# Attention's first gate projection ahead of the convolution's pointwise product, with TensorE's order planned from other durations

## The chip, the cores and the metric

The kernel runs on one core of one Trainium2 chip. The metric is the device time of one execution in microseconds, as the median of several runs; smaller is better.

## What is computed

A decoder trunk of two layers, on 256 positions of width 2048, all in float32. Each layer normalises its input, multiplies it by one combined projection matrix, and sends the columns of the result to three branches: a convolution module of 512 channels, a gated DeltaNet of 6 heads and a dilated windowed attention of 12 heads. Every branch has a gate of its own. The gated outputs together go through one output projection, which is added to the input.

```python
for l in range(DEPTH):
    h = rms_norm(x, norm_w[l])
    u = h @ w_in[l].astype(h.dtype)
    (c_in, c_gate, g_q, g_k, g_v, g_z, g_b, g_a,
     a_q, a_k, a_v, a_gate) = jnp.split(u, cuts, axis=-1)
    y_conv = conformer_conv(c_in, ..., conf_pw_w[l]) * jax.nn.silu(c_gate)
    y_gdn = gated_deltanet(g_q, g_k, g_v, g_z, g_b, g_a, ...)
    y_att = dilated_attention(a_q, a_k, a_v, cos, sin) * jax.nn.silu(a_gate)
    y = jnp.concatenate([y_conv, y_gdn, y_att], axis=-1)
    x = x + y @ w_out[l].astype(y.dtype)
return rms_norm(x, final_norm_w)

def conformer_conv(u, dw_w, dw_b, ln_w, ln_b, pw_w):
    a, b = jnp.split(u, 2, axis=-1)
    h = a * jax.nn.sigmoid(b)
    h = causal_dwconv(h, dw_w) + dw_b.astype(h.dtype)   # 31 taps
    h = layer_norm(h, ln_w, ln_b)
    h = jax.nn.silu(h)
    return h @ pw_w.astype(h.dtype)
```

The last line of `conformer_conv` is the pointwise product: 512 channels by 512. The DeltaNet's chunked rule solves a triangular system for each chunk of 64 positions (the kernel builds that inverse step by step, in the tile `inv`) and carries a state from chunk to chunk.

## The kernel before

**Projections.** Nearly all of TensorE's work is projection matmuls. Every float32 operand is split into a high and a low part, and a product is made of three matmuls (high by high, low by high, high by low). The normalised input lies in `HT` (high in HT0, low in HT1), 16 blocks of 128 channels; the input of the output projection and of the pointwise product lies in `YT` in the same way. Weights come by DMA on SyncE's queue into `raw` (4 buffers). ScalarE makes their high part `whi`, VectorE the low part `wlo` = raw - whi; each of these has 3 buffers. `unit` emits the matmuls of one block of 128 channels, 6 of them, or three for each 128 output columns in the channel-wise jobs ("chan"), in which the weights are the moving operand's partner and a matmul has 256 columns.

**Jobs.** `project` is one task that walks a list of jobs in a fixed order, the same in both layers: first the DeltaNet's and the convolution's input columns, then attention's q, k and v (AQ0 to AV1, of 384 columns each), the convolution's gate CG (512 columns), and at the layer's end the pointwise product and attention's two gate projections AG0 and AG1 (384 columns each, 144 matmuls); then the pieces of the output projection. A job accumulates in a pair of PSUM banks `acc`, of which there are two pairs, and when it is done a task is started that takes the result further (`conv_gate`, `conv_out`, `att_gate`).

**The convolution's chain.** Its taps run on VectorE as `scalar_tensor_tensor` instructions, one per tap and 128 channels (line 196 of the helper that records them). Then TensorE transposes the result, ScalarE and VectorE make mean and variance over channels (`lnst`), VectorE normalises, TensorE transposes back (tiles `b512_0` and `b512_1`), and ScalarE and VectorE apply scale, shift and swish and write the split result to the first four blocks of YT, in two halves of two blocks. Only then is the event `conf["pw"]` set, for which the pointwise product waits. The transposes are recorded at line 239 (`trs`), the other small matmuls of the chains at line 232 (`mms`).

**What sets the order.** All of it is written by generators ("tasks") that yield operations with an estimated duration: `("pe", cost, emit)` and so on. `Plan.run` is a list scheduler: it keeps a clock per engine, and of all the tasks' next operations it emits the one that can start first by the estimates, then by priority. The chip executes each engine's instructions in exactly this order; semaphores do the waiting. So the estimates decide where between the projection's matmuls the chains' small matmuls stand, and where between the weight splits VectorE's other instructions stand. The estimate's core is

```python
start = max(self.clock[o[0]], t.ready(o[0]))
key = (start, t.prio)
if best is None or key < best[0]:
    best = (key, t, o)
```

## Time and profile before

| what | value |
|---|---|
| median of 3 runs | 982.55 us (981.98 to 984.06) |
| the profiled execution's own time | 983.13 us |
| its span, first to last instruction | 981.4 us |
| mean granted TensorE clock | 0.991 |
| TensorE busy, matmuls | 959.3 us, 98% |
| VectorE busy | 758.6 us, 77% |
| ScalarE busy | 544.7 us, 56% |
| GpSimd busy | 57.4 us, 6% |

The span is that of one profiled execution; some 1.7 us of its time lie around it. The share of an engine is an average over the whole span: an engine at 77% can be full for a hundred microseconds and half empty elsewhere. A matmul's duration in the trace includes its way through the array, so that consecutive ones overlap; the pace is read from their starts. The granted clock is a share of 2.4 GHz, at its two levels 1.00 and 0.50 (1.2 GHz).

### The profile page before, as it was taken

The numbers are of one execution on the slowest core, as the hardware profiler recorded it, in microseconds if no ns is written. First come the engines' busy times: TensorE is split into PE (matmuls) and PEld (weight loads), VectorE is DVE, ScalarE is ACT, GpSimd is POOL, SyncE is SP. The second block draws the span as 40 slices with busy tenths as digits, with TensorE's granted clock in tenths as the row PEclk, the third lists the DMA queues.
The fourth block names the chain that finished last, engine by engine and source line by source line (L and its number), as shares of the span: only waits on it lengthen the run. The fifth ranks groups of instructions, "written<-read, shape, count | busy, mean of one in ns | idle before, by whom it ended". The sixth has DMA issues, their size and how long they took to land.

```text
span 981.4 us, 19748 instructions
## 1 busy us (share of the span) xinstructions
PE 959.3 (98%) x7595; PEld 937.9 (96%) x7595; DVE 758.6 (77%) x1473; ACT 544.7 (56%) x1061; POOL 57.4 (6%) x79
## 2 busy tenths in 40 slices
PE   8999999999999989999999999999999999899996
PEld 8999999999999979999899999999999999799996
DVE  7686799997999856655558768999989996666672
ACT  8764356445675665454456633564456656645551
POOL 1002000200110000000000020002001200100000
PEclk9999999999999979999999999999999999999998
DMA  9765555644445525777666555656344564467772
GB/s 335 255 215 155 184 192 181 187 145 148 150 141 186 186 65 181 223 241 222 215 200 198 197 163 172 192 179 199 124 142 152 163 201 148 131 194 222 228 251 86
DMA packets 67502, 180.31 MB, mean 184 GB/s; under 512 B 8016, under 2 KB 12240, under 8 KB 67408
## 3 DMA queue, kind: packets, MB, share of 16 engines
q1 hardware_dynamic: 64752, 174.08, 55.1%
q0 software_dynamic: 1712, 3.28, 1.3%
q10 hardware_dynamic: 944, 1.70, 0.5%
q8 instruction: 59, 0.97, 0.4%
q14 instruction: 35, 0.29, 0.1%
HBM read 173.26 MB, written 4.98 MB: 182 GB/s over the span
## 4 chain that ended last, share of the span: by engine, by line
PE 60%; DVE 1%; ACT 1%; issue 1%; ACTq 0%; POOLq 0%; POOL 0%; DVEq 0%
PE acc L454 54%; PE mix L232 3%; PE mix L239 2%; PE acc L463 1%; ACT b L191 0%; DVE b L196 0%; DVE wlo L199 0%; ACT JUNK L191 0%; ACT whi L191 0%; ACT YT L191 0%; DVE YT L199 0%; PE mix L753 0%; DVE inv L212 0%; DVE b L199 0%; ACTq L1064 0%
## 5 line engine op out<-in xcount | busy, mean ns | idle before, releaser
L454 PE MATMUL acc<-HT,whi 128*128 128x256 f32 x3072 | 541.7, 280 | 0.0
L191 ACT ACTIVATE whi<-raw 128x768 fp32r<-128x768 f32 (+4 forms) x389 | 340.1, 875 | 361.7 <-PE acc L454 311.2
L199 DVE TENSOR_TENSOR wlo<-raw,whi 128x768 fp32r<-128x768 f32 (+4 forms) x389 | 384.6, 989 | 167.1 <-ACT whi L191 163.6
L454 PEld LDWEIGHTS acc<-HT,whi 128*128 128x128 f32 x3072 | 466.4, 188 | 2.3 <-issue 1.8
L454 PE MATMUL acc<-HT,wlo 128*128 128x256 f32 x1536 | 426.7, 278 | 0.0
L454 PEld LDWEIGHTS acc<-HT,wlo 128*128 128x128 f32 x1536 | 288.6, 188 | 0.0
L454 PE MATMUL acc<-whi,YT 128*128 128x384 f32 (+2 forms) x640 | 161.8, 336 | 0.0
L196 DVE SCALAR_TENSOR_TENSOR b<-b,par,b 128x255 f32<-128x255 f32 (+20 forms) x348 | 151.9, 463 | 0.3
L454 PE MATMUL acc<-whi,HT 128*128 128x384 f32 (+1 forms) x512 | 134.6, 344 | 0.6 <-ACT whi L191 0.6
L454 PEld LDWEIGHTS acc<-whi,YT 128*128 128x128 f32 x640 | 114.0, 188 | 2.4
L454 PE MATMUL acc<-wlo,YT 128*128 128x384 f32 (+2 forms) x320 | 107.5, 336 | 0.0
L454 PEld LDWEIGHTS acc<-whi,HT 128*128 128x128 f32 x512 | 91.8, 190 | 1.3 <-ACT whi L191 1.2
L454 PE MATMUL acc<-wlo,HT 128*128 128x384 f32 (+1 forms) x256 | 87.2, 341 | 0.4 <-DVE wlo L199 0.4
L454 PEld LDWEIGHTS acc<-wlo,YT 128*128 128x128 f32 x320 | 60.1, 188 | 1.4
L454 PEld LDWEIGHTS acc<-wlo,HT 128*128 128x128 f32 x256 | 48.3, 189 | 1.1 <-DVE wlo L199 0.9
L232 PE MATMUL mix<-b,b 128*128 128x128 f32 (+5 forms) x456 | 47.3, 291 | 1.4 <-ACT b L191 1.4
L239 PE MATMUL mix<-ident,b 128*128 128x128 f32 x232 | 39.4, 290 | 7.2 <-DVE b L208 3.6
L232 PEld LDWEIGHTS mix<-b,b 128*128 128x128 f32 (+3 forms) x456 | 36.5, 163 | 8.6 <-ACT b L191 2.9
L239 PEld LDWEIGHTS mix<-ident,b 128*128 128x128 f32 x232 | 28.3, 147 | 11.2 <-DVE b L208 4.0
L191 ACT ACTIVATE b<-mix 128x384 f32<-128x384 f32 (+3 forms) x70 | 29.4, 436 | 16.9 <-PE mix L232 9.0
L196 DVE SCALAR_TENSOR_TENSOR b<-b,b 128x256 f32<-128x256 f32 (+3 forms) x62 | 31.5, 510 | 5.5 <-ACT b L191 5.4
L191 ACT ACTIVATE JUNK<-b 128x128 bf16<-128x128 f32 (+3 forms) x62 | 25.0, 403 | 16.2 <-DVE b L199 11.0
(148 smaller groups left out, 642.1 us busy)
## 6 DMA issues: line engine op xcount, KB each, us to landing
raw<-in_w_in SPq DMA_DIRECT2D x240, 384.0 KB
raw<-in_w_in SPq DMA_DIRECT2D x48, 512.0 KB
raw<-in_w_out SPq DMA_DIRECT2D x64, 384.0 KB
raw<-in_w_out SPq DMA_DIRECT2D x12, 512.0 KB
raw<-in_w_in SPq DMA_DIRECT2D x15, 396.0 KB
b<-in_x SPq DMA_DIRECT2D x10, 256.0 KB
raw<-in_conf_pw_w SPq DMA_DIRECT2D x4, 512.0 KB
raw<-in_w_out SPq DMA_DIRECT2D x8, 256.0 KB
```

The source lines that it names most:

```text
L191: lambda: nc.scalar.activation(out_, in_, func, bias=bias, scale=scale, **kw))
L196: lambda: nc.vector.scalar_tensor_tensor(out_, a, s, b, op0=op0, op1=op1))
L199: return ("dve", 70 + _free(out_) / 0.96, lambda: nc.vector.tensor_tensor(out_, a, b, op=op))
L232: nc.tensor.matmul(o, a, b, start=f[0], stop=f[1])
L239: nc.tensor.transpose(o, a, ident)
L454: nc.tensor.matmul(o, w, m, start=first and i == 0 and not (chan and t % 2), stop=last and i == 2, skip_group_check=chan)
L463: nc.tensor.matmul(acc[t][:, :n], YT[w][:, k, s], HT[m][:, k, :n], start=k == 0 and i == 0, stop=k == KB - 1 and i == 2)
```

## The change

Two things are changed. In the job list, attention's gate projection AG0 moves ahead of the pointwise product, so that a layer ends with CG, AG0, pointwise product, AG1, where it had CG, pointwise product, AG0, AG1. And the estimated durations of TensorE's operations are other ones: a projection unit of 384 columns counts 1035 or 1038 ns where it counted 975, a transpose costs 109 ns and 100 for the group where it cost 107, and a group of small matmuls is estimated by its columns and partitions. Nothing of what is computed changes, nor the number of instructions.

```diff
--- before.py
+++ after.py
@@ -230,14 +230,18 @@
             for o, a, b, *f in jobs:
                 f = f or (True, True)
                 nc.tensor.matmul(o, a, b, start=f[0], stop=f[1])
-        cost = sum(max(53.0, 4 * max(_free(j[1]), _free(j[2])) / 2.4) for j in jobs)
-        return ("pe", cost, emit)
+        def one(a, b):
+            n = max(_free(a), _free(b))
+            if n <= 64:
+                return 30.0 if n <= 32 else 58.0
+            return 2 * n / 2.4 * (0.5 if min(a.shape[0], _free(a)) <= 64 else 1.0) + 4.0
+        return ("pe", 100.0 + sum(one(j[1], j[2]) for j in jobs), emit)
 
     def trs(*jobs):
         def emit():
             for o, a in jobs:
                 nc.tensor.transpose(o, a, ident)
-        return ("pe", 107.0 * len(jobs), emit)
+        return ("pe", 100.0 + 109.0 * len(jobs), emit)
 
     def summax(out_, a, b, mx):
 
@@ -453,7 +457,7 @@
                 for i, (w, m) in enumerate(terms):
                     nc.tensor.matmul(o, w, m, start=first and i == 0 and not (chan and t % 2), stop=last and i == 2,
                                      skip_group_check=chan)
-        return ("pe", 6 * (n / 2.4 + 2.5), emit)
+        return ("pe", n // 128 * 3 * 115.0 if chan else 6 * (n / 2.4 + 13.0), emit)
 
     def last_unit(acc, t, k, n):
 
@@ -462,7 +466,7 @@
             for i, (w, m) in enumerate(((0, 0), (1, 0), (0, 1))):
                 nc.tensor.matmul(acc[t][:, :n], YT[w][:, k, s], HT[m][:, k, :n], start=k == 0 and i == 0,
                                  stop=k == KB - 1 and i == 2)
-        return ("pe", 3 * (n / 2.4 + 2.5), emit)
+        return ("pe", 3 * (n / 2.4 + 13.0), emit)
 
     def project(jobs):
 
@@ -1264,9 +1268,9 @@
             inp(AV + 384 * i, 384, heads_in(i), 7)
         inp(CG, 512, conv_gate, 6, True)
         cs_ready = [conf["pw"]] * KB
+        inp(AG, 384, att_gate(0), 6, True)
         jobs.append((YT, cs_ready, wpw, 0, 512, full[:2], conv_out, 6, None, True))
-        for i in range(2):
-            inp(AG + 384 * i, 384, att_gate(i), 6, True)
+        inp(AG + 384, 384, att_gate(1), 6, True)
         for j, (c0, n) in enumerate(pieces):
             mode = "last" if last and j == len(pieces) - 1 else False
             jobs.append((YT, y_ready, wout, c0, n, [(4 * i, 4) for i in range(4)] if mode else full, (last_residual if last else residual)(j),
```

Since the estimates set the order, the change moves instructions on all engines. Three places are shown.

TensorE, end of layer 0, before: the group of transposes of `b512_0` and `b512_1` (the normalised convolution output) that stands last ahead of the pointwise product, whose matmuls read YT0 and YT1. Ahead of these rows stand the transposes of the first half, and ahead of them CG's last matmul.

```order
L232 MATMUL mix3_126<-b384_2_111,b768_1_91 64x256
L232 MATMUL mix3_126<-b384_3_112,b768_1_91 64x256
L232 MATMUL mix3_126<-b384_2_111,b768_1_91 64x128
L232 MATMUL mix3_126<-b384_3_112,b768_1_91 64x128
L239 MATMUL mix2_125<-ident_139,b512_0_107 128x128
L239 MATMUL mix2_125<-ident_139,b512_1_108 128x128
L239 MATMUL mix2_125<-ident_139,b512_0_107 128x128
L239 MATMUL mix2_125<-ident_139,b512_1_108 128x128
L454 MATMUL acc10_129<-YT0_76,whi2_85 128x256
L454 MATMUL acc10_129<-YT1_77,whi2_85 128x256
L454 MATMUL acc10_129<-YT0_76,wlo2_88 128x256
```

After the change, the transposes stand inside AG0 (matmuls that read HT), the first group 63 of its 144 matmuls in, the second group 117 in:

```order
L458 MATMUL acc11_130<-HT1_75,whi2_85 128x256
L458 MATMUL acc11_130<-HT0_74,wlo2_88 128x256
L243 MATMUL mix2_125<-ident_139,b512_0_107 128x128
L243 MATMUL mix2_125<-ident_139,b512_1_108 128x128
L243 MATMUL mix2_125<-ident_139,b512_0_107 128x128
L243 MATMUL mix2_125<-ident_139,b512_1_108 128x128
L458 MATMUL acc10_129<-HT0_74,whi2_85 128x256
L458 MATMUL acc10_129<-HT1_75,whi2_85 128x256
```

```order
L458 MATMUL acc11_130<-HT1_75,whi2_85 128x256
L458 MATMUL acc11_130<-HT0_74,wlo2_88 128x256
L243 MATMUL mix1_124<-ident_139,b512_0_107 128x128
L243 MATMUL mix1_124<-ident_139,b512_1_108 128x128
L243 MATMUL mix1_124<-ident_139,b512_0_107 128x128
L243 MATMUL mix1_124<-ident_139,b512_1_108 128x128
L458 MATMUL acc10_129<-HT0_74,whi2_85 128x256
```

and the pointwise product begins right behind AG0's last matmul:

```order
L458 MATMUL acc11_130<-HT0_74,whi0_83 128x256
L458 MATMUL acc11_130<-HT1_75,whi0_83 128x256
L458 MATMUL acc11_130<-HT0_74,wlo0_86 128x256
L458 MATMUL acc00_127<-YT0_76,whi1_84 128x256
L458 MATMUL acc00_127<-YT1_77,whi1_84 128x256
L458 MATMUL acc00_127<-YT0_76,wlo1_87 128x256
```

What moved: the pointwise product stands 144 matmuls further behind CG, and between the second group of transposes and its first matmul there are now 27 of AG0's matmuls where there was none.

VectorE, middle of layer 1, before: weight splits (`wlo`), steps of the DeltaNet's inverse (`inv` and the product `b_3` beside it, 48 partitions, at the steps of 16 to 14 rows) and taps of the short convolution (`b_5`, `par`):

```order
L199 TENSOR_TENSOR wlo_86<-raw_81,whi_83 128x768
L199 TENSOR_TENSOR b_3_118<-inv_121,inv_120 48x255
L196 SCALAR_TENSOR_TENSOR b_2_117<-b_5_95,par_150,b_2_117 128x253
L199 TENSOR_TENSOR wlo_87<-raw_78,whi_84 128x768
L199 TENSOR_TENSOR inv_120<-inv_120,b_3_118 48x15x17
L196 SCALAR_TENSOR_TENSOR b_3_93<-b_5_95,b_2_117 128x256
L199 TENSOR_TENSOR b_3_118<-inv_121,inv_120 48x252
L196 SCALAR_TENSOR_TENSOR b_0_115<-b_5_95,par_150,b_0_115 128x255
L199 TENSOR_TENSOR wlo_88<-raw_79,whi_85 128x768
L199 TENSOR_TENSOR inv_120<-inv_120,b_3_118 48x14x18
```

After, at the same three splits (the same buffers `raw_81`, `raw_78` and `raw_79`):

```order
L199 TENSOR_TENSOR wlo_86<-raw_81,whi_83 128x768
L199 TENSOR_TENSOR b_3_118<-inv_121,inv_120 48x207
L196 SCALAR_TENSOR_TENSOR b_2_117<-b_5_95,par_150,b_2_117 128x253
L199 TENSOR_TENSOR inv_120<-inv_120,b_3_118 48x9x23
L196 SCALAR_TENSOR_TENSOR b_0_115<-b_5_95,par_150,b_0_115 128x255
L199 TENSOR_TENSOR wlo_87<-raw_78,whi_84 128x768
L199 TENSOR_TENSOR b_3_118<-inv_121,inv_120 48x192
L196 SCALAR_TENSOR_TENSOR b_3_93<-b_5_95,b_2_117 128x256
L199 TENSOR_TENSOR inv_120<-inv_120,b_3_118 48x8x24
L199 TENSOR_TENSOR wlo_88<-raw_79,whi_85 128x768
L199 TENSOR_TENSOR b_3_118<-inv_121,inv_120 48x175
```

What moved: the inverse is at its steps of 9 to 7 rows at the place where it was at 15 and 14, and between the first and the third of these splits stand seven other instructions where there were six. Counted over the whole stretch from GQ0's first split to AQ0's last there are 213 VectorE instructions where there were 193 in layer 0, and 218 where there were 191 in layer 1. The DeltaNet's small matmuls on TensorE stand some 9 us of projection matmuls earlier in layer 0, and 14 to 19 us earlier in layer 1.

VectorE, layer 1, the end of AV1: before, the splits of CG's first chunks (`wlo` of 128x1024) with the convolution's last taps (`par`, 128x226) between them:

```order
L196 SCALAR_TENSOR_TENSOR b_0_104<-b_1_105,par_150,b_0_104 128x226
L199 TENSOR_TENSOR wlo_88<-raw_81,whi_85 128x1024
L196 SCALAR_TENSOR_TENSOR b_0_104<-b_1_105,par_150,b_0_104 128x226
L196 SCALAR_TENSOR_TENSOR b_12_102<-b_3_93,b_12_102 128x768
L199 TENSOR_TENSOR wlo_86<-raw_78,whi_83 128x1024
L196 SCALAR_TENSOR_TENSOR b_0_104<-b_1_105,par_150,b_0_104 128x226
L199 TENSOR_TENSOR wlo_87<-raw_79,whi_84 128x1024
L196 SCALAR_TENSOR_TENSOR b_0_104<-b_1_105,par_150,b_0_104 128x226
```

After:

```order
L196 SCALAR_TENSOR_TENSOR b_0_104<-b_1_105,par_150,b_0_104 128x226
L199 TENSOR_TENSOR wlo_87<-raw_80,whi_84 128x768
L196 SCALAR_TENSOR_TENSOR b_0_104<-b_1_105,par_150,b_0_104 128x226
L196 SCALAR_TENSOR_TENSOR b_12_102<-b_0_90,b_12_102 128x768
L199 TENSOR_TENSOR wlo_88<-raw_81,whi_85 128x1024
L196 SCALAR_TENSOR_TENSOR b_0_104<-b_1_105,par_150,b_0_104 128x226
L196 SCALAR_TENSOR_TENSOR b_7_97<-b_7_97,sso_197,b_12_102 128x128 x2
L199 TENSOR_TENSOR wlo_86<-raw_78,whi_83 128x1024
```

What moved: the last tap stands right behind the split of CG's first chunk, where it stood behind that of the third. On TensorE the transposes that read its result stand 90 matmuls into AV1, six from its end, where they stood 144 matmuls into CG.

## Rows read from the trace of the kernel before

**Rows 1.** The page, busy time, share of the span and instructions per engine.

```profile
PE 959.3 (98%) x7595; PEld 937.9 (96%) x7595; DVE 758.6 (77%) x1473; ACT 544.7 (56%) x1061; POOL 57.4 (6%) x79
```

**Rows 2.** TensorE's timeline, end of layer 0: start, duration, operation, [idle before, releaser].

```profile
349.01 0.28 PE L454 MATMUL acc<-HT,wlo 128*128 128x256 f32 x1
352.25 0.48 PE L239 MATMUL mix<-ident,b 128*128 128x128 f32 x1 [2.97 <-DVE b L206]
353.01 2.24 PE L239 MATMUL mix<-ident,b 128*128 128x128 f32 x9 [0.28 <-ACT b L191]
355.18 1.54 PE L232 MATMUL mix<-b,b 128*64 128x256 f32 x8
356.66 1.11 PE L239 MATMUL mix<-ident,b 128*128 128x128 f32 x4
358.41 1.31 PE L454 MATMUL acc<-YT,whi 128*128 128x256 f32 x2 [0.64 <-ACT YT L191]
...
362.06 0.28 PE L454 MATMUL acc<-YT,wlo 128*128 128x256 f32 x1
```

**Rows 3.** Windows there: length, each engine's busy time, granted clock, DMA share.

```profile
352.00:354.00 2.00, 1.46 (x6) 0.98 (x7) 1.82 (x4) 1.86 (x5) 0.00 (x0) 0.50 0.55 187
360.00:362.00 2.00, 2.00 (x11) 2.00 (x11) 1.30 (x2) 0.63 (x1) 0.00 (x0) 0.50 0.00 0
362.00:364.00 2.00, 2.00 (x19) 2.00 (x18) 0.54 (x2) 0.85 (x1) 0.00 (x0) 1.00 0.00 0
```

**Rows 4.** TensorE's timeline, end of layer 1.

```profile
835.42 0.28 PE L454 MATMUL acc<-HT,wlo 128*128 128x256 f32 x1
837.87 0.33 PE L239 MATMUL mix<-ident,b 128*128 128x128 f32 x1 [2.17 <-DVE b L208]
839.64 1.99 PE L239 MATMUL mix<-ident,b 128*128 128x128 f32 x9 [1.44 <-DVE b L208]
...
844.09 0.54 PE L454 MATMUL acc<-YT,whi 128*128 128x256 f32 x2
...
847.49 0.38 PE L454 MATMUL acc<-YT,whi 128*128 128x256 f32 x1 [0.36 <-ACT YT L191]
848.22 0.39 PE L454 MATMUL acc<-YT,whi 128*128 128x256 f32 x1 [0.34 <-DVE YT L199]
```

**Rows 5.** The chain of waits, layer 1: start, duration, what, how many.

```profile
769.79 10.42 PE acc L454 x90
...
782.93 0.80 PE mix L232 x8
```

**Rows 6.** VectorE's timeline, end of layer 0.

```profile
352.11 0.54 DVE L208 TENSOR_SCALAR b<-b,lnst 128x512 f32<-128x512 f32 x1
...
361.34 0.69 DVE L199 TENSOR_TENSOR YT<-b,YT 128x512 fp32r<-128x512 f32 x1 [0.69 <-ACT YT L191]
```

**Rows 7.** Windows in the middle of each layer, columns as in the other windows.

```profile
108.20:206.30 98.10, 98.10 (x914) 97.73 (x913) 93.21 (x200) 51.08 (x100) 5.58 (x9) 1.00 0.58 183
593.40:692.70 99.30, 99.30 (x914) 98.91 (x914) 93.52 (x200) 51.12 (x98) 5.43 (x9) 1.00 0.59 184
```

**Rows 8.** The page's costliest groups: busy us, mean ns of one | idle before.

```profile
L196 DVE SCALAR_TENSOR_TENSOR b<-b,par,b 128x255 f32<-128x255 f32 (+20 forms) x348 | 151.9, 463 | 0.3
```

**Rows 9.** VectorE's timeline in the middle of layer 0.

```profile
137.78 0.96 DVE L199 TENSOR_TENSOR wlo<-raw,whi 128x768 fp32r<-128x768 f32 x1
138.65 0.40 DVE L199 TENSOR_TENSOR inv<-inv,b 48x247 f32<-48x247 f32 x1
```

**Rows 10.** VectorE's timeline, layer 1, around CG's first weight split.

```profile
804.12 1.21 DVE L199 TENSOR_TENSOR wlo<-raw,whi 128x1024 fp32r<-128x1024 f32 x1
805.26 0.44 DVE L196 SCALAR_TENSOR_TENSOR b<-b,par,b 128x226 f32<-128x226 f32 x1
...
809.13 0.44 DVE L196 SCALAR_TENSOR_TENSOR b<-b,par,b 128x226 f32<-128x226 f32 x1
```

**Rows 11.** TensorE's timeline, layer 1, CG's first matmuls.

```profile
806.34 0.40 PE L454 MATMUL acc<-HT,whi 128*128 128x256 f32 x2
```

## The prediction

> **What bounds the kernel now.** I read the page's busy shares first: TensorE 98% of the span, VectorE 77%, ScalarE 56% [rows 1]. With TensorE that full, time can only come out of the stretches in which it idles or runs at its lower clock, so the second view was TensorE's timeline, searched for places where one instruction starts much later than its forerunner allows. Two stand out, one at the end of each layer. In layer 0 the last matmul of the convolution gate CG starts at 349.01; the pointwise product's first is at 358.41, and the usual pace is back only at 362.06 [rows 2]. The reader is to see two things there: 2.97 us of idle ahead of a transpose, and then small matmuls and pointwise matmuls that take twice their time. The windows say why: a granted clock of 0.50 from 352 to 362 (1.2 GHz), and 1.00 (2.4 GHz) from 362 [rows 3]. The engine had been idle before the fall, and the clock rose again only after some 3.6 us of pointwise matmuls. In layer 1 the same stretch runs from 835.42 to 848.22, with its own waits at 837.87, 839.64, 847.49 and 848.22 [rows 4]. No other wait on TensorE stands out beside these two.
>
> The usual pace is 10.42 / 90 = 0.116 us for a 256-column matmul, and 0.80 / 8 = 0.10 us for a small one [rows 5].
>
> **What the stall costs.** Layer 0: TensorE is done with CG at 349.01 + 0.12 = 349.13, and 12.93 us pass until 362.06. In them stand 14 pointwise matmuls (14 x 0.116 = 1.62) and 22 small ones (2.2 at the full clock), which have to be done anyway. Lost: 12.93 - 1.62 - 2.20 = 9.1 us. Layer 1: from 835.54 to 848.22 are 12.68 us, with 25 pointwise matmuls (2.90) and the same 22 small ones. Lost: 7.6 us. Together **16.7 us**, the most that the swap can return.
>
> **Part 1, the swap.** 144 matmuls of AG0 (16.7 us) now stand between CG and the pointwise product, in both layers; AG0 reads the normalised input and waits for nothing new. What the pointwise product waits for is the LayerNorm chain: TensorE's transposes, then ScalarE and VectorE up to the low half of YT. In layer 0 both normalised halves are there at 352.11 + 0.54 = 352.65 [rows 6]. By the order their transposes now stand 63 and 117 matmuls into AG0. These come at 349.13 + 63 x 0.116 + about 1.4 for the small ones ahead = 357.8, and at about 364.5: no wait at either. From the second transposes to the last low half it took 362.03 - 356.66 = 5.4 us [rows 2, 6], hence 364.5 + 5.4 = 369.9 (up to 370.4, since VectorE and ScalarE now also split AG0's weights). AG0 ends at 349.13 + 16.7 + 2.2 = 368.0, and the pointwise product wants YT's second half after 24 matmuls, at 370.8. The cost lies between 0 and 1 us; I take 0.5. TensorE idles nowhere long enough to lose its clock, so the whole 9.1 goes. Nothing is late next: AG1 (16.7 us) now follows the pointwise product and covers the convolution's gating ahead of the output product, which is two more passes of this kind (under 5.4 us).
>
> The Trainium skill (TensorE: Matmul & The Clock Gate, Back-to-back issue gap) gives an isolated matmul columns / 2.4 + 2.5 ns, which is exactly the old estimate and by which it needed no correction: 109.2 ns for 256 columns, an estimate from that page of 15.7 us for AG0. By it the last wait would be about 1.5 us instead of 0.5. The trace has 116 ns for these pairs of load and matmul, so the new estimate of 115 is the one that it bears out.
>
> **Part 2, the estimates.** They cost nothing to execute; they only re-order. Old estimates let the planner's TensorE run about 6% too fast (109 against 116 ns), so chain work was put later in TensorE's order than it could have been. With the new ones the planner fits more chain work beside each matmul: the Gated DeltaNet's chains stand some 9 us earlier in layer 0 and 14 to 19 us earlier in layer 1, and VectorE gets more instructions between the same weight splits. From GQ0's first split to AQ0's last (44 splits) VectorE has 213 instructions where it had 193 in layer 0, and 218 where it had 191 in layer 1.
>
> That is where the change can cost, since VectorE is nearly full there and TensorE does not wait: 93.21 of 98.10 us and 93.52 of 99.30, with TensorE busy throughout [rows 7]. The added instructions are mostly taps, 463 ns each [rows 8]; a following instruction starts 0.08 before the one ahead ends (137.78 + 0.96 = 138.74, next at 138.65) [rows 9], so 0.39 net. Layer 0: 20 x 0.39 = 7.8 us, against 4.9 idle and the lead of the splits. That lead is about one chunk, since WLO has three buffers and a chunk is 18 matmuls (2.1 us). Layer 1: 27 x 0.39 = 10.5 against 5.8 idle and 2.1. At face value 0.8 + 2.6 = 3.4 us by which splits come late to TensorE. Bounds: 0, if VectorE closes up further than the rows show; 18.3, if neither idle time nor lead can be used. I take **4.0**, near the face value and a little above it, as not every idle moment lies where it is wanted.
>
> The Trainium skill (Perfetto Trace Analysis, Identifying the Most-Contended Engine) calls occupancy a fair measure of headroom for VectorE, but not for TensorE's matmuls. By it the 95% would be the whole truth, and the sum would have 3.4 here. No row shows yet whether the last 5% can be used.
>
> In layer 1 the convolution's chain is moved too: its transposes stand 90 matmuls into AV1, before 144 into CG. TensorE comes there at about 805.3, as CG's first pairs start at 806.34 [rows 11]. The last tap on VectorE now stands right behind the split of CG's first chunk, which ended at 804.12 + 1.21 = 805.3 [rows 10]; before, it started at 809.13. So a wait of 0.5 to 2 us, at most 809.57 - 805.3 = 4.3 if VectorE gets no further than before, and 0 if it runs ahead. I take 1.0. Everything behind it in layer 1 (LayerNorm's transposes 84 into CG and 9 into AG0) has 20 us and more until the pointwise product, so the 7.6 goes.
>
> **Sum.** 983.13 (the profiled execution) - 16.7 + 0.5 + 4.0 + 1.0 = 971.9. The median lies 0.58 lower: **971.3 us**.
>
> **The rivals.**
> *VectorE absorbs it all.* The last wait and the late splits come to nothing: 983.13 - 16.7 - 0.58 = 965.9. For it: only 3.4 of 18.3 are uncovered at face value. Against: VectorE at 95%, and the wait in AV1. Chance 0.14.
> *The wait in layer 1 only moves.* VectorE, with one more instruction per split, reaches the last tap no sooner than before. TensorE idles 4.3 us in AV1, longer than the 3.1 us after which layer 0's clock was at 0.50; that clock held for 3.6 to 10 us [rows 2, 3], of which half is lost: 1.8 to 5. Some 7.7 in place of my 1.0: 978.0. Chance 0.09.
> *Slower: VectorE becomes the bound in mid-layer.* The 47 added instructions find neither idle time nor lead, TensorE waits 18.3 instead of 4.0, and the time is 985.6. It outweighs the gain as soon as less than 18.3 - 15.2 = 3.1 of the 14.9 us of idle time and lead is usable. For it: idle time scattered in bits behind ScalarE's results. Against: the splits' lead evens such bits out. Chance 0.07.
> *No change.* The chain's transposes make TensorE wait inside AG0 as long as they did ahead of the pointwise product. Against: 352.65 is 5 us before they are wanted. About 982.5, chance 0.04.
>
> **How the numbers follow.** My forecast has 0.66, with a range of its own of 968 to 975. Within 0.2% (some 2 us, about what a measurement of this kernel tells from no change) is only the last rival, with the edges of its neighbours 0.04; slower 0.07; faster 0.89. For 8 in 10 the range reaches down to the case in which everything is absorbed and up over the one whose wait moves: 965.5 to 979.5. It leaves out the slower rival, no change, and about 0.06 of the edges.
>
> **What would show it.** Right: no TensorE idle above 1 us between CG and the pointwise product, granted clock 1.00 through both layer ends, AG0's 144 matmuls ahead of the product at 0.116 each. The 4.0 shows as TensorE waits on VectorE's wlo or on the DeltaNet's inverse, within the two mid-layer windows, with VectorE's busy share above 95%; the 1.0 as a wait for VectorE at the transposes in AV1; the 0.5 as one at the product's third block. Wrong: a long idle in AV1 with a half clock behind it, or waits on wlo that repeat every chunk.

## The result and the profile after

The changed kernel takes 971.17 us (median of 4 runs, 968.40 to 971.72), beside 983.01 us of the kernel before (4 runs, 981.98 to 984.06): 0.987 of it, with an interval of 0.985 to 0.990. That is 1.3% faster, and 0.1 us from the forecast of 971.3. The sum came out, but not every term of it did; the trace and the experiments show which.

The page's first part, busy time per engine (the profiled execution took 971.46 us):

```profile
span 969.4 us, 19752 instructions
...
PE 953.4 (98%) x7595; PEld 932.8 (96%) x7595; DVE 757.2 (78%) x1483; ACT 541.9 (56%) x1051; POOL 57.4 (6%) x79
```

No engine has become lighter to speak of, beside [rows 1]; the same work stands 12 us closer together. TensorE's timeline at the end of layer 0 answers to [rows 2]:

```profile
350.36 0.28 PE L458 MATMUL acc<-HT,wlo 128*128 128x256 f32 x1
350.47 0.39 PE L458 MATMUL acc<-HT,whi 128*128 128x256 f32 x2
...
359.33 0.60 PE L243 MATMUL mix<-ident,b 128*128 128x128 f32 x4
...
365.90 0.60 PE L243 MATMUL mix<-ident,b 128*128 128x128 f32 x4
...
369.42 0.39 PE L458 MATMUL acc<-YT,whi 128*128 128x256 f32 x2
...
372.14 0.28 PE L458 MATMUL acc<-YT,whi 128*128 128x256 f32 x1
372.89 0.38 PE L458 MATMUL acc<-YT,whi 128*128 128x256 f32 x1 [0.48 <-DVE YT L199]
```

CG's last matmul is at 350.36 and AG0's first 0.11 us later. Both groups of LayerNorm's transposes run without a wait, and the product begins behind AG0 without one. What is left is one wait of 0.48 for the low half of YT, at the product's third block, 372.89 - 369.42 = 3.5 us in; VectorE writes that half last in this chain:

```profile
372.16 0.68 DVE L199 TENSOR_TENSOR YT<-b,YT 128x512 fp32r<-128x512 f32 x1
```

The windows there and in the middle of the layers answer to [rows 3] and [rows 7] (columns as there). The last two lie between the same projection matmuls as the windows of [rows 7]:

```profile
350.00:352.00 2.00, 2.00 (x20) 2.00 (x19) 1.90 (x5) 2.00 (x6) 0.00 (x0) 1.00 0.67 184
360.00:362.00 2.00, 2.00 (x20) 2.00 (x19) 0.23 (x1) 2.00 (x4) 0.00 (x0) 1.00 0.69 223
...
108.69:210.79 102.10, 102.10 (x968) 100.74 (x967) 99.99 (x218) 53.08 (x104) 5.45 (x9) 1.00 0.57 176
585.56:689.91 104.35, 104.32 (x987) 102.65 (x986) 100.86 (x215) 54.08 (x107) 6.20 (x10) 1.00 0.56 172
```

The granted clock stays at 1.00 (2.4 GHz). In the middle of the layers the same 743 or 744 projection matmuls now take 102.10 and 104.35 us, where they took 98.10 and 99.30: the moved chains bring small matmuls of TensorE with them, 222 and 240 where there were 168 in either layer, and TensorE still has next to no idle there. VectorE is busy for 99.99 of the 102.10 us and 100.86 of the 104.35, where it was for 93.21 of 98.10 and 93.52 of 99.30. Last, the list of what TensorE waited for in the whole span (releaser, us in total, times, longest):

```profile
PE mix L232 <- ACT b L191: 2.5, 2, 1.8
PE mix L321 <- POOL pw_neg L326: 1.6, 1, 1.6
PE mix L243 <- DVE b L196: 1.4, 1, 1.4
PE acc L458 <- DVE wlo L199: 0.9, 3, 0.4
PE acc L458 <- DVE YT L199: 0.5, 1, 0.5
PE acc L458 <- ACT whi L191: 0.5, 1, 0.5
```

The 1.6 is at the start, and so is all but 0.2 of the waits for `wlo` and `whi`; none of them lies in the two windows. The 1.4 for VectorE is the wait at the convolution's transposes in AV1. The largest, 2.5 for ScalarE, is a wait that the prediction did not have.

To see where time goes between kernels whose projection matmuls run in the same job order but for the swap, it is read between two matmuls that have the same projection work between them. Two such stretches carry nearly everything: from GQ0's first matmul to CG's first (the middle of a layer), and from CG's last matmul to AG1's first (the layer's end: AG0, the pointwise product and the small matmuls that the order puts there). Differences of start times in TensorE's timelines, us:

| kernel | layer 0 middle | layer 0 end | layer 1 middle | layer 1 end |
|---|---|---|---|---|
| before | 212.88 | 34.02 | 213.22 | 31.84 |
| changed | 213.54 | 25.35 | 214.61 | 25.70 |
| changed, a second profile | 213.49 | 25.27 | 213.72 | 25.70 |
| swap alone | 212.89 | 26.42 | 213.22 | 24.71 |
| estimates alone | 214.96 | 33.13 | 213.49 | 25.84 |
| swap, units' estimate | 216.53 | 24.24 | 218.86 | 24.28 |
| swap, small ones' estimates | 212.48 | 30.21 | 211.57 | 27.21 |
| small ones' estimates from the trace | 213.44 | 24.24 | 214.90 | 24.24 |
| changed, rotation's DMAs from GpSimd | 211.44 | 25.27 | 213.13 | 25.70 |
| swap, rotation's DMAs from GpSimd | 210.97 | 26.50 | 212.40 | 24.74 |

Before to changed: -8.67 and -6.14 at the ends, +0.66 and +1.39 in the middles, +0.7 elsewhere, together -12.0 us.

Two things besides waits move these numbers. The orders put 14 to 30 small matmuls into a layer's end (22 in both layers before). And a projection matmul has one of two paces, 113 or 118 ns from start to start (see the last section), which makes some 0.9 us on the 192 of a layer's end. The kernel before has 118 in layer 0's end and 113 in layer 1's, the changed kernel 113 and 118, the swap alone 113 in both. So of the 8.67 some 0.9 is pace, and the 6.14 lacks as much; the sum of the two, 14.8, is free of it.

### The profile page after: what moved, and what is told of

It is laid out like the page before. It is cut to its first block, busy times and chain, and to the rows that moved or that the text cites. A ratio compares the mean times of both kernels' runs of the same rounds, so it can differ in the third digit from the quotient of the medians.

```text
span 969.4 us, 19752 instructions
## 1 busy us (share of the span) xinstructions
PE 953.4 (98%) x7595; PEld 932.8 (96%) x7595; DVE 757.2 (78%) x1483; ACT 541.9 (56%) x1051; POOL 57.4 (6%) x79
## 5 line engine op out<-in xcount | busy, mean ns | idle before, releaser
L196 DVE SCALAR_TENSOR_TENSOR b<-b,par,b 128x254 f32<-128x254 f32 (+20 forms) x348 | 151.4, 465 | 0.3
L243 PE MATMUL mix<-ident,b 128*128 128x128 f32 x232 | 36.6, 274 | 1.4 <-DVE b L196 1.4
L191 ACT ACTIVATE b<-b 128x256 f32<-128x256 f32 (+3 forms) x52 | 27.7, 540 | 6.9 <-DVE b L196 4.0
```

Source lines behind the costliest of these rows:

```text
L191: lambda: nc.scalar.activation(out_, in_, func, bias=bias, scale=scale, **kw))
L196: lambda: nc.vector.scalar_tensor_tensor(out_, a, s, b, op0=op0, op1=op1))
L243: nc.tensor.transpose(o, a, ident)
```

## The experiments

**The swap alone.** The job order of the change, the old estimates.

```diff
         cs_ready = [conf["pw"]] * KB
+        inp(AG, 384, att_gate(0), 6, True)
         jobs.append((YT, cs_ready, wpw, 0, 512, full[:2], conv_out, 6, None, True))
-        for i in range(2):
-            inp(AG + 384 * i, 384, att_gate(i), 6, True)
+        inp(AG + 384, 384, att_gate(1), 6, True)
```

> The job order of the change with the old estimates. In TensorE's order LayerNorm's transposes then stand 63 and 117 matmuls into AG0 in layer 0, as after the change, and 72 and 108 into AG0 in layer 1. Theory (the swap returns the stall at both layer ends, the estimates only cost): faster than the changed kernel; by the prediction's terms 983.1 - 16.7 + 0.5 = 966.9, by the idle time that the two traces show (15.1 us gone at the two layer ends, 2.5 more lost elsewhere) 968.0 to 968.5. Rival (the estimates are needed for part of the gain, by bringing the chains forward): slower than the changed kernel, 973 or more.

Measured: 969.24 us (968.10 to 970.17), 0.985 of before (0.983 to 0.988). The theory held, with the time 0.7 us above the range from the traces and 2.3 above the prediction's terms: the whole gain is there without the estimates. Both layers' ends give it (-7.60 and -7.13), the middles stay as they were to 0.01 us. In layer 0 the product waits for YT twice, 0.83 and 0.62 us, where the changed kernel waits 0.48 once; the estimates help there, and cost elsewhere.

**The estimates alone.** The same piece of the diff undone in the changed kernel.

> The new estimates with the old job order CG, pointwise product, AG0, AG1. In layer 0 both groups of LayerNorm's transposes still stand right ahead of the pointwise product, so its stall stays whole; in layer 1 the first group now stands 84 matmuls into CG and only the second right ahead of the product, so that about 5.4 - 24 x 0.116 = 2.6 us of waiting remain of some 7. Theory (estimates cost 2.5 to 5.0 elsewhere, and return some 4 to 5 at layer 1's end): 980.5 to 983.5, no change that can be told. Rival (the estimates give a good part of the gain by themselves): 977 or less.

Measured: 978.27 us (976.65 to 978.42), 0.994 of before (0.992 to 0.996), faster than the theory's range and slower than the rival's. Layer 0's end keeps its stall, as expected: it is 0.9 us shorter, about what the faster of the two paces, which it has here, makes. Layer 1's loses nearly all that the two together take (-6.00 against -6.14, or against some -7.0 at equal pace), where I had expected 2.6 us to stay. TensorE's timeline there has one wait:

```profile
837.39 1.31 PE L243 MATMUL mix<-ident,b 128*128 128x128 f32 x10
839.54 0.87 PE L232 MATMUL mix<-b,b 128*64 128x256 f32 x8 [0.84 <-ACT b L191]
```

So in layer 1 the parts of the change are two ways to nearly the same gain, and it is counted once; in layer 0 only the swap has it. The second half of YT is not waited for, most likely because LayerNorm's second group, by its size the first four of the ten transposes at 837.39, does not stand last ahead of the product as I had it: six transposes and eight small matmuls with their wait stand between, and the product, which begins at 840.34, wants that half at about 843.1, 5.7 us behind the group, where the chain took 5.4 in the kernel before. In the middle of layer 0 this kernel lost its clock behind a wait that the changed kernel has too (last section), which is a part of the 214.96.

**The swap with the projection units' estimate alone.**

```diff
-        return ("pe", 6 * (n / 2.4 + 2.5), emit)
+        return ("pe", n // 128 * 3 * 115.0 if chan else 6 * (n / 2.4 + 13.0), emit)
...
-        return ("pe", 3 * (n / 2.4 + 2.5), emit)
+        return ("pe", 3 * (n / 2.4 + 13.0), emit)
```

> The swap with the new estimate of the projection units alone; transposes and small matmuls keep their old ones. The planner now takes TensorE for slower than it is wherever small matmuls are many, and puts the convolution's transposes some 200 matmuls (23 us) further ahead in both layers (layer 0: 2148 projection matmuls in instead of 2352). [...] Rival (only the projection's estimate matters, and VectorE keeps up): 968 to 972, no new wait.

Measured: 977.23 us (974.96 to 979.13), 0.994 of before (0.992 to 0.996). It is slower than the changed kernel by 6 us, as forecast (974 to 985), and not within the rival's range. TensorE has new waits at transposes, for VectorE and for ScalarE. The layers' ends are as short as any (24.24 and 24.28, 2.2 and 0.4 less than in the swap alone), and the middles, +3.7 and +5.6, pay more than that returns. TensorE's list of waits is longer and spread over the chains; its first three rows:

```profile
PE mix L232 <- ACT b L191: 2.2, 1, 2.2
PE acc L454 <- DVE wlo L199: 1.8, 3, 1.3
PE mix L239 <- DVE b L196: 1.8, 2, 1.1
```

The granted clock stays at 1.00 at all of these waits. The projection's estimate made right, with the small operations' old ones beside it, is worse here than the old table, in which the projection's was too short.

**The swap with the small operations' estimates alone** (the diff's pieces for `mms` and `trs`, the units as before).

> The swap with the new estimates of transposes and small matmuls alone; the projection units keep the old, 6% too short ones. The planner's TensorE is then faster than the chip's everywhere, chain work stands later: LayerNorm's second transposes right ahead of the pointwise product in both layers. Theory (a second group right ahead of the product leaves 5.4 - 2.8 = 2.6 us of waiting per layer, and nothing else is worse than with the swap alone): 973 to 974. Rival (the place of the transposes within AG0 does not matter): as the swap alone.

Measured: 973.90 us (971.86 to 974.48), 0.990 of before (0.987 to 0.992), as the theory had it. The middles cost nothing, but the layers' ends return only 3.81 and 4.63: the second group of transposes stands right ahead of the product, which waits for its result. It does matter where within AG0 the transposes stand.

**The pointwise product behind both gate projections.**

```diff
-        inp(AG, 384, att_gate(0), 6, True)
+        for i in range(2):
+            inp(AG + 384 * i, 384, att_gate(i), 6, True)
         jobs.append((YT, cs_ready, wpw, 0, 512, full[:2], conv_out, 6, None, True))
-        inp(AG + 384, 384, att_gate(1), 6, True)
```

> The changed kernel with the pointwise product behind both of attention's gate projections: CG, AG0, AG1, product. LayerNorm's chain then has 33 us of cover, and the wait of 0.64 at the product's third block goes. But conv_out (gate, high part, low part: some 2.1 us for the first half by the durations of such passes, 0.7 each) now has no cover, since the output product reads the convolution's blocks first. Theory (what AG1 covers in the changed kernel is worth about 2 us per layer): 974 to 976. Rival (conv_out is covered anyway): 970 to 971.

Measured: 982.94 us (979.55 to 984.96), 0.999 of before (0.997 to 1.000): the whole gain is gone. The theory's direction was right and its size far too small. TensorE's timeline at the step from the product to the output projection, and a window behind it:

```profile
390.99 0.28 PE L458 MATMUL acc<-YT,wlo 128*128 128x256 f32 x1
393.21 0.44 PE L458 MATMUL acc<-whi,YT 128*128 128x384 f32 x1 [1.95 <-ACT YT L191]
395.44 0.69 PE L458 MATMUL acc<-whi,YT 128*128 128x384 f32 x1 [1.79 <-DVE YT L199]
```

The window behind it:

```profile
396.00:398.00 2.00, 2.00 (x8) 2.00 (x7) 0.48 (x1) 0.00 (x0) 0.00 (x0) 0.50 0.35 138
```

VectorE's timeline between the product's end and that second matmul, where the operations of 128x512 are `conv_out`'s and those of 128x256 belong to AG1's gating:

```profile
391.18 0.68 DVE L196 SCALAR_TENSOR_TENSOR b<-acc,b 128x512 f32<-128x512 f32 x1
391.78 0.41 DVE L199 TENSOR_TENSOR b<-b,b 128x256 f32<-128x256 f32 x1
392.11 0.95 DVE L199 TENSOR_TENSOR wlo<-raw,whi 128x768 fp32r<-128x768 f32 x1
392.98 0.41 DVE L196 SCALAR_TENSOR_TENSOR YT<-b,YT 128x256 fp32r<-128x256 f32 x1
393.31 0.68 DVE L196 SCALAR_TENSOR_TENSOR b<-acc,b 128x512 f32<-128x512 f32 x1
393.92 0.41 DVE L196 SCALAR_TENSOR_TENSOR b<-b,b 128x256 f32<-128x256 f32 x1
394.36 0.43 DVE L199 TENSOR_TENSOR b<-b,b 128x256 f32<-128x256 f32 x1
394.70 0.68 DVE L199 TENSOR_TENSOR YT<-b,YT 128x512 fp32r<-128x512 f32 x1
```

The wait is 3.7 us and not 2.1, since AG1's gating and a weight split stand among `conv_out`'s steps, and the granted clock falls to 0.50 behind it, so that the output projection's matmuls start at half their pace. Layer 1 has the same waits (1.73 and 1.79), and the clock is at 0.50 from 394.5 to 401.3 and from 882.6 to 886.0. Waits of 7.3 us and half of 10.2 us make 12.4, an estimate that meets the 11.8 us by which this kernel is slower than the changed one. AG1 behind the product is worth about as much as AG0 ahead of it: the place in the middle is the one that covers both chains.

**The kernel before, with TensorE kept at work.**

```diff
             acc = yield ("get", ACC)
+            if A is YT and chan is True:
+                yield ("pe", 0.0, lambda: [nc.tensor.transpose(acc[0][:, :128], ones, ident) for _ in range(20)])
...
                     yield ("wait", ready[k])
+                    if A is YT and chan is True and i + a == 0:
+                        yield ("pe", 0.0, lambda: [nc.tensor.transpose(acc[0][:, :128], ones, ident) for _ in range(16)])
```

> The kernel before with idle matmuls of TensorE put into its stall: 20 transposes of a constant right behind CG's last matmul and 16 right ahead of the pointwise product, in both layers, written to a bank that the product overwrites. They wait for nothing, so that TensorE should keep its higher clock. It splits the 16.7 us of the stall into what the half clock costs and what waiting for the chain costs. Theory (the chain sets the stall; at the higher clock its transposes and small matmuls are some 1 to 1.5 us sooner per layer, and the pointwise product waits for YT's second half all the same): 980 to 981.5. Rival (the half clock is most of the stall): 976 or less.

Measured: 981.46 us (980.11 to 982.62), 0.998 of before (0.997 to 0.999). The windows at the places of [rows 3] now have the full clock:

```profile
352.00:354.00 2.00, 0.79 (x6) 0.40 (x4) 2.00 (x6) 1.86 (x4) 0.07 (x1) 1.00 0.79 212
360.00:362.00 2.00, 2.00 (x19) 1.92 (x17) 1.30 (x2) 1.34 (x2) 0.00 (x0) 1.00 0.00 0
```

and the layers' ends are 1.82 and 0.11 us shorter. So of the stall (16.7 us by the prediction, 14.7 by what the swap alone returns) some 2 come back with the full clock, and the rest is the chain of transposes, ScalarE and VectorE that the product waits for. A remedy had to cover the chain; holding the clock alone would not have done.

**More work for VectorE in the middle of the layers.** The added result is read by nothing; where `SCR` and `loaded` are made is left out.

```diff
-        yield tt(lo, view, hi.bitcast(F32), ALU.subtract)
+        op = tt(lo, view, hi.bitcast(F32), ALU.subtract)
+
+        def emit():
+            op[2]()
+            if i in loaded:
+                nc.vector.tensor_tensor(SCR, SCR, SCR, op=ALU.add)
+        yield (op[0], op[1], emit)
...
```

> The changed kernel with one additional VectorE instruction (a constant tile of 128x192 added to itself, about 0.27 us net) behind each of the 44 weight splits from GQ0's first to AQ0's last, in both layers: 11.9 us of work per layer, at the place where VectorE is fullest. TensorE's order is unchanged. Nothing reads the added result. Theory (idle time of 1.5 and 2.1 us and a lead of 2.1 per layer are usable, the rest comes late to TensorE): 11.9 x 2 - 7.8 = 16 us longer, 987. The slower rival's premise (neither idle time nor lead is usable): 24 us longer, 995. The other premise (VectorE has more room than the windows show, since what is late there is caught up behind): 971 to 977.

Measured: 988.16 us (986.41 to 989.61), 17.0 longer than the changed kernel, as the theory of partly usable room had it (16). The 88 instructions took 0.346 us each by the trace, some 0.27 net of the 0.08 by which neighbours overlap, 23.8 us in all; about 7 of them found room, where I had counted 7.8. The list of TensorE's waits shows where most of the rest came out, in its first row:

```profile
PE mix L243 <- DVE b L196: 12.8, 15, 2.0
```

The changed kernel has 1.4 in that row. Not at the weight splits, as I had pictured it, but at transposes that wait for taps: by this list the splits have a lead, and a tap whose result is transposed next has none. Here TensorE's order and its number of matmuls stay as they were, so that the stretch does not grow with the added work as it does in the change itself. The Trainium skill (Perfetto Trace Analysis, Identifying the Most-Contended Engine) calls occupancy a fair measure of VectorE's headroom; this run agrees with it, since at 98% of its window VectorE handed on 17 of 23.8 added microseconds.

**The small operations' estimates from the trace.**

```diff
-            return 2 * n / 2.4 * (0.5 if min(a.shape[0], _free(a)) <= 64 else 1.0) + 4.0
-        return ("pe", 100.0 + sum(one(j[1], j[2]) for j in jobs), emit)
+            return 4 * n / 2.4 * (0.7 if min(a.shape[0], _free(a)) <= 64 else 1.0)
+        return ("pe", 30.0 + sum(one(j[1], j[2]) for j in jobs), emit)
...
-        return ("pe", 100.0 + 109.0 * len(jobs), emit)
+        return ("pe", 30.0 + 103.0 * len(jobs), emit)
```

> The changed kernel with the estimates of the small operations set to what the trace shows for them: a transpose 103 ns and 30 for the group, a small matmul of 128 columns 213 ns (each is executed as two instructions), of 64 rows 0.7 of that. Planner and chip then agree on TensorE through the attention stretch, where the changed kernel's planner falls 10 us behind the chip's clock per layer. The convolution's transposes move ahead by another 156 projection matmuls in layer 0 and 78 in layer 1, LayerNorm's to before CG's end. Theory (what a correct table buys is nothing where TensorE has no waits left, and earlier transposes wait for VectorE): 972 to 977. Rival (the waits left in the changed kernel come from the wrong table): 966 to 969.

Measured: 969.78 us (968.70 to 969.99), 0.986 of before (0.985 to 0.988): between the theory's range and the rival's, and not to be told from the changed kernel. The convolution's transposes stand earlier, and yet VectorE is there: the wait in AV1 falls to 0.25 and 0.13, the layers' ends come to 24.24 in both layers, and other small waits take the place of that, the longest 0.79 for VectorE.

**The changed kernel and the swap alone, side by side**, with two more, on one chip.

> The changed kernel itself once more, beside the next three on the same chip, to compare it with the swap alone: 971.

> The swap alone with the old estimates once more, beside the changed kernel. Theory (the estimates cost 2 to 3 us, as the traces' idle time has it): 968.5 to 969.5, some 2 below the changed kernel. Rival (the two are equal, and the difference of the first runs was one of chips): within 0.7 of the changed kernel.

Measured: changed 970.43 us (969.74 to 971.14), swap alone 968.96 (968.26 to 970.02). The swap alone is 1.5 us ahead, 0.15%, less than what I called told from no change; that the estimates cost a little is likely by the two traces and not settled by the times. No run shows that they bring anything beside the swap.

**The rotation's DMAs from GpSimd.** ScalarE's timeline in the changed kernel, ahead of the wait of 1.8 us:

```profile
230.00 1.24 ACTq L1067 DMA_DIRECT2D b<-b  x1
231.27 0.64 ACTq L1068 DMA_DIRECT2D b<-b  x1
231.94 0.63 ACTq L1067 DMA_DIRECT2D b<-b  x1
232.60 0.63 ACTq L1068 DMA_DIRECT2D b<-b  x1
233.34 0.31 ACT L191 ACTIVATE JUNK<-b 128x128 bf16<-128x128 f32 x1 [2.49 <-DVE b L196]
```

ScalarE issues four small DMAs for attention's rotation, 3.2 us. A weight split that it had begun runs beside the first of them, and from 230.85 to 233.34 it executes nothing; the activations of the DeltaNet's state stand behind the issues, and TensorE waits for those from 234.16 to 236.00. The row names VectorE's `b` as what ended the idle; the run below shows that it was not that.

```diff
-                        nc.scalar.dma_start(sh[p:p + 8], buf[p + 8:p + 16])
-                        nc.scalar.dma_start(sh[p + 8:p + 16], buf[p:p + 8])
+                        nc.gpsimd.dma_start(sh[p:p + 8], buf[p + 8:p + 16])
+                        nc.gpsimd.dma_start(sh[p + 8:p + 16], buf[p:p + 8])
```

> The changed kernel with the four small DMAs of attention's rotation issued by GpSimd and no longer by ScalarE; TensorE's order is unchanged. In the changed kernel ScalarE issues them from 230.00 to 233.2 ahead of the DeltaNet state's activations, for which TensorE then waits 2.0 us at 233.9. Theory (that wait is ScalarE's time in issuing): 2.0 us in layer 0 and part of 0.8 in layer 1 go, 968.5 to 969. Rival (the wait moves to the next link of the state's chain, or GpSimd's issue comes later): within 0.7 of the changed kernel.

> The swap alone, with the rotation's DMAs issued by GpSimd. Its waits on TensorE lie elsewhere (1.13 at 243.1, 0.48, 0.53, 0.77, 0.55, and 1.9 at the pointwise product). Theory (ScalarE's issuing is behind the wait at 243.1 too): 0.5 to 1.5 less than the swap alone, 967.5 to 968.5. Rival (no wait of this kernel hangs on it): as the swap alone.

Measured: the changed kernel so edited 967.21 us (966.89 to 967.68), 3.2 below the changed kernel on the same chip; the swap alone so edited 966.82 (966.43 to 967.75), 2.1 below the swap alone. Both are faster than either kernel of this study, and both gained more than the theories' ranges had. With the issues on GpSimd, the same activation follows on the split at once:

```profile
228.68 0.54 POOL L1067 DMA_DIRECT2D b<-b  x1 [9.17 <-ACT JUNK L191]
230.39 0.29 ACT L191 ACTIVATE JUNK<-b 128x128 bf16<-128x128 f32 x1
```

The list of TensorE's waits in the first of the two has no row for ScalarE's `b` any more:

```profile
PE mix L321 <- POOL pw_neg L326: 1.6, 1, 1.6
PE mix L243 <- DVE b L196: 1.4, 1, 1.4
PE acc L458 <- DVE wlo L199: 0.6, 2, 0.4
PE acc L458 <- DVE YT L199: 0.5, 1, 0.5
PE acc L458 <- ACT whi L191: 0.4, 1, 0.4
```

That is 2.5 us of waits gone; the rest of the 3.2 was not traced to a place. With the DMAs out of the way the two orders are 0.4 us apart, too little to tell. That fits a cost of the estimates which is mostly that they put the state's chain further behind ScalarE's issuing, but as that cost itself is not settled by the times, this is not shown.

## Why the prediction was right, and where it was not

- **The stall at the layers' ends, 16.7 us, of which all but 0.5 goes.** Right in kind, and too large by 1.4 in all: 14.8 went where 16.2 was forecast. In layer 0 the end is 8.67 us shorter, against 9.1 - 0.5 = 8.6 forecast, but 0.9 of that is the faster pace, so that the agreement is luck; in layer 1 it is 6.14 against 7.6, with as much lost to the slower pace. The swap alone has 22 small matmuls and no wait in layer 1's end: 24.71 - 192 x 0.1133 = 2.95 us for them, where the sum had 2.2 (0.10 each). That is 0.75 per layer of work that the sum counted as stall, and makes the 1.4, roughly. The small matmuls that the changed order adds there (26 for 22) cost little.
- **The wait at the product's third block, 0.5 in a range of 0 to 1.** It is there, at that place and for that releaser, with 0.48. The working would have given none: it had the chain of 5.4 us ready 0.4 us and more before the product wants it. Everything stands 1.4 us later than worked out, the second transposes (365.90) as well as the product, but the chain behind them took 6.9 us, to 372.84, with splits of the product's and AG1's weights and AG0's gating between its steps on VectorE and ScalarE. The allowance was right, its size is luck.
- **The half clock.** That TensorE would no longer lose its clock at the layers' ends is so; that it idles nowhere long enough for it is less sure than it was put (last section). The prediction did not say how much of the stall was the clock; it is some 2 us, by the run that kept TensorE at work.
- **The mid-layer cost, 4.0.** The step that failed. "At face value 0.8 + 2.6 = 3.4 us by which splits come late to TensorE": none did in the two windows. The sum set VectorE's added work against a stretch that stays 98.10 or 99.30 us long. But the moved chains bring TensorE's small matmuls too, 54 and 72 more, and the same projection work with its 44 splits (which end in the middle of AQ0; its last is the 48th) now takes 4.0 and 5.1 us longer, without an idle. VectorE's busy time grew by 6.8 and 7.3 us (7.8 and 10.5 were worked out): 9.1 of these 14.1 us found room in the longer stretch and 5.1 in VectorE's idle time. The longer stretch costs nothing by itself, as these matmuls are gone from a later place: from GQ0's first to CG's first there are 378 small ones in layer 0, before and after. The term that was paid instead is ScalarE's issuing of DMAs, 2.5 us of waits, which the prediction overlooked although the kernel before had the same wait in smaller form (0.97 us at 244.00, behind the same four DMAs, and 0.40 in layer 1). A moved chain has to be followed past the DMA issues on every queue it crosses, ScalarE's among them.
- **The wait in AV1, 1.0 in a range of 0 to 4.3.** There, with 1.44 us in one profile of the changed kernel and 0.68 in the second.
- **The new estimates.** That the old pace was too fast was read rightly, though 0.116 itself was not: the 10.42 us of [rows 5] reach to the end of the last of the 90 matmuls, and their starts lie 113 to 114 ns apart. The step from there was too simple. The new unit estimate alone makes the kernel slower than the swap with the old one by 8 us; it needs the small operations' estimates beside it, and these are too short for the wide ones: a group of three of 128 columns counts 432 ns and takes some 690 in the trace (236.00 to 236.69). Better numbers for them changed nothing that the times can tell.
- **The rivals.** The slower one, that VectorE has no room left, did not come about in this change, but its mechanism is real where TensorE's order stays as it is: 24 us of added work lengthened the kernel by 17.
- **The total.** 16.2 and 5.0 were forecast to net 11.2; 14.8 and 2.1 and 0.7 elsewhere net 12.0 by the traces. Two errors of opposite sign, 1.4 too much gain and some 2.2 too much cost, left the forecast near the median; the closeness is luck.

## What to carry to other kernels

Where a chain is late at a product, look for independent work of the same engine that can stand between, and place it so that the chain behind the product stays covered too: AG0 ahead and AG1 behind returned 12 us, both ahead returned none. When a chain moves, count what it brings to every engine: the stretch that gets VectorE's added work also gets TensorE's, and grows by it. A planner's estimates work as a set; one that was made right beside the old others made the kernel slower (977 instead of 969 us), and no set that was tried was faster than the old one with the swap. And before a scheduling edit, list the DMA issues on compute engines: four small ones took ScalarE 3.2 us in one piece, and moving them to an idle engine was worth 2 to 3 us, more than the choice between the old and the new estimates.

## What was not expected of the hardware

The same matmul has two paces at the full granted clock. AG1's 144 matmuls of 256 columns, with no other matmul and no wait between them, take 16.97 us in layer 0 and 16.33 in layer 1 of the kernel before, as the starts of AG1's first and of the output projection's first matmul show in TensorE's timelines:

```profile
383.02 0.40 PE L454 MATMUL acc<-HT,whi 128*128 128x256 f32 x2
...
399.99 0.34 PE L454 MATMUL acc<-whi,YT 128*128 128x384 f32 x1
...
867.26 0.39 PE L454 MATMUL acc<-HT,whi 128*128 128x256 f32 x2
...
883.59 0.33 PE L454 MATMUL acc<-whi,YT 128*128 128x384 f32 x1
```

That is 118 and 113 ns each, and every other kernel here in which AG1 stands at that place has one or the other, kept through the stretch. Within longer unbroken runs at the full clock no trace has the pace change; it changes where TensorE waited, ran small matmuls or went to another width. The changed kernel had 16.97 for layer 0's stretch in one profiled execution and 16.32 in another. With some 4,700 such matmuls the two paces lie some 20 us apart if one held throughout (an estimate), so a part of what executions of one kernel differ by may come from here. What decides between the two was not found. The Trainium skill (TensorE: Matmul & The Clock Gate, Back-to-back issue gap) has 109.2 ns for an isolated matmul of 256 columns, as an estimate from its formula; both paces lie above it.

The same wait took the clock along in one kernel and not in another. Ahead of the state's matmuls in layer 0 TensorE waits 1.84 us for ScalarE in the changed kernel (to 236.00) and in the kernel with the estimates alone (to 235.91). Behind it the granted clock is 1.00 in the first, and 0.50 in the second from 236.1 to 239.5, of which half is lost:

```profile
236.00:238.00 2.00, 2.00 (x17) 2.00 (x18) 2.00 (x4) 1.17 (x2) 0.00 (x0) 1.00 0.26 81
...
236.00:238.00 2.00, 2.00 (x10) 2.00 (x11) 2.00 (x4) 1.08 (x2) 0.00 (x0) 0.52 0.33 60
```

So a wait of this length can cost the clock or not, and that the changed kernel's did not in two profiles was not to be foreseen from the rows. What decides it is open too.
